# Dilated attention: transposing q and k whole and splitting them out of PSUM, with the second stack of q written by DMA

## The chip, the core and the metric

The kernel runs on one core of a Trainium2 chip. The metric is the device time of one launch in microseconds. A core has five engines with instruction queues of their own: TensorE (PE; PEld is its weight load), VectorE (DVE), ScalarE (ACT), GpSimd (POOL) and SyncE (SP), which here only issues DMAs. Each engine works through its queue in order and waits there for what an instruction needs.

## The reference

Two layers of an encoder over 1024 rows of 1024 numbers in fp32: latent attention with an MLP, then dilated attention with an MLP. The change lies in the dilated attention:

```python
proj = (h @ w_in).reshape(B, S, N_DIL_GROUPS, 3, DIL_HEADS, DIL_HEAD_DIM)   # 3 groups, 16 heads of 64
for gi, (window, dilation) in enumerate(DIL_GROUPS):      # (128, 1), (512, 4), (2048, 16)
    q = rms_norm(proj[:, :, gi, 0], g_q[gi])              # norm over the 64 numbers of a head
    k = rms_norm(proj[:, :, gi, 1], g_k[gi])
    v = proj[:, :, gi, 2]
    o, lse = dilated_group(q, k, v, pos, table, window, dilation)
...
wts = jax.nn.softmax(jnp.stack(lses, axis=0), axis=0)
o = jnp.einsum('gbsh,gbshd->bshd', wts.astype(o_all.dtype), o_all)
```

Within a group a row attends to 64 rows at each side of it (at the distance of the dilation), with a bias per head and distance. The results of the three groups are merged with the denominators of their softmaxes.

## The kernel before, in words

**The stage.** The dilated stage is the method `dil`. It goes through the three groups, in each through eight pairs of heads (a pair is a unit), and in each unit through four steps `tp`; a step makes q and k of two tiles of 128 rows for the pair. That makes 96 steps. Between two groups one empty step permutes the activations for the next dilation (`permute`, copies on ScalarE, VectorE and GpSimd).

**Precision.** A product in nearly full fp32 is made from halves: x is written as hi + lo, both in the type fp32r, hi being x rounded to it and lo the rest. A projection takes three matmuls per block (hi hi, hi lo, lo hi; lines 414 to 416). The scores use stacks instead: for one head the 128 partitions of a tile hold 64 rows of hi and 64 rows of lo. Matmul 0 multiplies the stack of k (hi over lo) with a stack of q that has hi over lo, matmul 1 with one that has lo over hi. Their sum in PSUM has all four products.

**One step, before.** `project` makes the two tiles of q and k of the pair (psproj; 48 matmuls for a tile). `qkstep` forms the norm: squares on ScalarE (dsq, L1825), the sum on VectorE, then qn = psproj times the reciprocal root. On qn, 128x512 (tile, then q of head 0 and 1, then k of head 0 and 1), VectorE multiplies the q half by the product of the two norm weights (gain, L1832). ScalarE copies hi into the first third of `st` (L1834), VectorE writes lo into the second (L1835), and GpSimd copies the q part of hi into the last (L1838), so that hi, lo, hi lie side by side. One step later `stacks` takes windows of 128 columns from it: hi|lo is one stack, lo|hi the other. TensorE transposes them, eight of q (psq, L1847) and four of k (psk, L1855), and ScalarE copies the results to SBUF: two tiles `q` (L1850) and a stretch of `kT` (L1856), which holds the key stacks of the unit.

**After the stacks.** `scores` (L1878) multiplies the q stacks of a tile with 256 key columns around it, four matmuls a tile, into pss; SP loads the tile's bias for it (`bt`, three buffers, L1871). A tile can be scored once the keys behind it are there, so in a unit the two tiles 2 tp - 1 and 2 tp come ready with step tp. VectorE adds the bias and takes the maximum, ScalarE takes the exponential (pd, L1889), `ptrans` transposes the probabilities (pspt, L1904) into pT hi (ScalarE, L1906) and lo (VectorE, L1907), and `av` multiplies with V (psav, L1919 and 1920) and adds up into U on VectorE (L1921, a TENSOR_REDUCE).

**What goes beside.** SP loads weights of two units ahead (wqkr, four loads of 256 KB a unit, L1547) which ScalarE and VectorE split into wqkh (L121) and wqkl (L122) in front of each unit; V is loaded and split per two units. In the third group, when a unit ends, SP brings the U of the first two groups back (`um`, L2024, eight DMAs) and VectorE merges (`merge`, L1989 and 1991, ten instructions); `emit` transposes the merged U (psot, L2008) one step later and stores it to oTd. Where the stage ends, oT is loaded again from oTd for the output projection.

**What orders it.** The Python loop above the step writes out, in this order: V of the step before (`av`), the split of the coming weights, the projection of the first tile, `ptrans`, the um loads, `scores`, `stacks` of two steps back, `emit`, the projection of the second tile, `qkstep`. A list scheduler of the framework then fixes the order on each engine's queue from the dependences; at run time an engine doesn't leave that order. Tiles in PSUM come from one pool of eight banks (psD).

Of the kernel before, what the change touches and what calls it, by code (L numbers as in the profile page):

```python
# [9 lines left out]
F32 = mybir.dt.float32  # L10
F32R = mybir.dt.float32r
# [3 lines left out]
AF = mybir.ActivationFunctionType  # L15
ALU = mybir.AluOpType
# [4 lines left out]
P = 128  # L21
D = 1024
S = 1024
# [18 lines left out]
class K:  # L42
# [1702 lines left out]
    def dil(self, at0, at1, tail, wqk, vd):  # L1745


        nc, a, tc = self.nc, self.a, self.tc
        ctx = ExitStack()
        mkp = lambda name, bufs: ctx.enter_context(tc.tile_pool(name=name, bufs=bufs, reuse_waits="tile"))  # L1750
        dpool = mkp("dil", 2)
        psp = ctx.enter_context(tc.tile_pool(name="psD", bufs=8, space=PSUM, reuse_waits="tile"))
        D_ = lambda name, shape, dt, bufs: dpool.tile(list(shape), dt, tag=name, bufs=bufs, name=self.nm(name))
        PS = lambda name, dt=F32: psp.tile([P, 512], dt, tag="b", name=self.nm(name))
        identr = dpool.tile([P, P], F32R, name="identr", bufs=1)
        nc.vector.tensor_copy(identr, self.ident)
# [62 lines left out]
        def qkstep(u, tp, ps):  # L1819

            g = u["g"]
            p8 = ps.rearrange("p (n e) -> p n e", e=64)
            sq = self.T("dsq")
            ms = self.sm("dms", 8)
            nc.scalar.activation(sq, ps, AF.Square, scale=0.125)  # L1825
            nc.vector.tensor_reduce(ms, sq.rearrange("p (n e) -> p n e", e=64), op=ALU.add, axis=AX.X)
            r = self.rstd(ms, 8, "dr")
            qn = self.T("qn")
            q8 = qn.rearrange("p (n e) -> p n e", e=64)
            nc.vector.tensor_tensor(q8, p8, r.unsqueeze(2).broadcast_to([P, 8, 64]), op=ALU.mult)  # L1830
            qq = qn.rearrange("p (i n e) -> p i n e", i=2, e=64)[:, :, 0:2, :]
            nc.vector.tensor_tensor(qq, qq, gain[:, g : g + 1, :].unsqueeze(1).broadcast_to([P, 2, 2, 64]), op=ALU.mult)  # L1832
            st = D_("st", (P, 8, 192), F32R, 1)
            nc.scalar.activation(st[:, :, 0:64], q8, AF.Copy)  # L1834
            nc.vector.tensor_tensor(st[:, :, 64:128], q8, st[:, :, 0:64].bitcast(F32), op=ALU.subtract)  # L1835
            s4 = st.rearrange("p (i n) e -> p i n e", i=2)
            for i in range(2):
                nc.gpsimd.tensor_scalar(s4[:, i, 0:2, 128:192], s4[:, i, 0:2, 0:64].bitcast(F32), 1.0, 1.0,  # L1838
                                        op0=ALU.mult, op1=ALU.mult)
            return s4  # L1840

        def stacks(u, tp, s4):
            for i in range(2):
                ps = PS("psq", F32R)
                for e in range(2):
                    for k in range(2):
                        nc.tensor.transpose(ps[:, (2 * e + k) * P : (2 * e + k + 1) * P],  # L1847
                                            s4[:, i, e, 64 * k : 64 * k + 128], identr)
                q = D_("q", (P, 2, 2, P), F32R, 4)
                nc.scalar.activation(q.rearrange("p e k t -> p (e k t)"), ps.bitcast(F32), AF.Copy)  # L1850
                u["q"][2 * tp + i] = q
            ps = PS("psk", F32R)
            for e in range(2):
                for i in range(2):
                    nc.tensor.transpose(ps[:, (2 * e + i) * P : (2 * e + i + 1) * P], s4[:, i, 2 + e, 0:128], identr)  # L1855
            nc.scalar.activation(u["k"][:, :, 2 * tp * P : (2 * tp + 2) * P],  # L1856
                                 ps.rearrange("p (e t) -> p e t", e=2).bitcast(F32), AF.Copy)

        def span(g, t):
            if g == 2:  # L1860
                return 64, 192
            n = 8 if g == 0 else 2
            return 64 if t % n == 0 else 0, 192 if t % n == n - 1 else 256

        def scores(u, t):
            g, pr = u["g"], u["pr"]
            bt = D_("bt", (P, 2, 256), F32, 3)
            idx = self.even * (8 - t) + t
            src = self.bias[g][bass.ds(idx, 1), 2 * pr : 2 * pr + 2, 0 : P * 256]
            b0, b1 = (64, 192) if g == 2 else (0, 256)  # L1870
            nc.sync.dma_start(out=bt[:, :, b0:b1], in_=src.rearrange("o h (q c) -> q (o h) c", c=256)[:, :, b0:b1])  # L1871
            ps = PS("pss")
            w0 = min(max(P * t - 64, 0), S - 256)
            off = w0 - (P * t - 64)
            q = u["q"].pop(t)
            for e in range(2):
                for k in range(2):
                    nc.tensor.matmul(ps[:, e * 256 : (e + 1) * 256], q[:, e, k, :], u["k"][:, e, w0 : w0 + 256],  # L1878
                                     start=k == 0, stop=k == 1)
# [7 lines left out]
            nc.scalar.activation(nb, stat[:, g, t, 0, 2 * pr : 2 * pr + 2], AF.Identity, scale=-1.0, bias=ln14)  # L1887
            for e in range(2):
                nc.scalar.activation(p[:, e, lo:hi], p[:, e, lo:hi], AF.Exp, bias=nb[:, e : e + 1],  # L1889
                                     accum_out=stat[:, g, t, 1, 2 * pr + e : 2 * pr + e + 1])  # L1890
# [201 lines left out]
        for n, step in enumerate(steps):  # L2092
# [14 lines left out]
            if step is not None:  # L2107
                kind, g, pr, tp = step
                w = wts[(kind, g, pr)]
                if tp == 0:  # L2110
                    units[(g, pr)] = {"g": g, "pr": pr, "q": {}, "V": VSs[(g, pr // 2)],
                                      "k": D_("kT", (P, 2, S), F32R, 2), "U": self.G("U", (P, 8, P), F32)}
                u = units[(g, pr)]
            for x in transposed:
                x[0]["at"] = n
# [2 lines left out]
            if step is not None:  # L2118
                ps = PS("psproj")
# [197 lines left out]
```

## Time and profile before

| | |
|---|---|
| time, median of 3 runs | 3377.55 us (3376.37 to 3378.83) |
| profiled execution, as a run | 3372.89 us |
| its span, first to last instruction | 3371.0 us |
| its mean granted TensorE clock | 0.985 |
| VectorE, ScalarE, GpSimd busy in the span | 74%, 56%, 23% |
| transposes of `st` (first to last) | 1686.7 to 2626.4 us |

A profile shows one execution. The busy lines of the page give, for each engine, busy time, its share of the span and the number of instructions. A row of a group says: line, engine, operation, tile written <- tiles read, shape and type, count | busy time, mean ns of one | idle time of the engine just ahead of them and what ended most of it; rows of the view by tile say min/median/max ns, first and last start, form. A row of the timeline gives start, length, engine, line, operation, count and, in brackets, the wait ahead of it. A row of a chain of waits gives start, length, engine, tile and line: the chain that ended last, followed back from the end. A row by windows gives a stretch, its length, the busy time of PE, PEld, VectorE, ScalarE and GpSimd, then the granted clock, the share of the 16 DMA engines and GB/s.

### The profile page before, as it was taken

The numbers are of one execution on the slowest core, as the hardware profiler recorded it, in microseconds if no ns is written. First come the engines' busy times: TensorE is split into PE (matmuls) and PEld (weight loads), VectorE is DVE, ScalarE is ACT, GpSimd is POOL, SyncE is SP. The second block draws the span as 40 slices with busy tenths as digits, with TensorE's granted clock in tenths as the row PEclk, the third lists the DMA queues.
The fourth block names the chain that finished last, engine by engine and source line by source line (L and its number), as shares of the span: only waits on it lengthen the run. The fifth ranks groups of instructions, "written<-read, shape, count | busy, mean of one in ns | idle before, by whom it ended". The sixth has DMA issues, their size and how long they took to land.

```text
span 3371.0 us, 53254 instructions
## 1 busy us (share of the span) xinstructions
PE 3250.1 (96%) x19046; PEld 2794.4 (83%) x19046; DVE 2480.3 (74%) x4492; ACT 1877.2 (56%) x3798; POOL 767.5 (23%) x1173
## 2 busy tenths in 40 slices
PE   6989999999999999899999999999999799999999
PEld 6877677688887888778899989998999688887887
DVE  6677777648877866787677787777888578778666
ACT  5547777835544434532267787777667355444342
POOL 6455565520111000011222232222211001110000
PEclk9999999999999999999999999999999899999999
DMA  5453232253655796456433333343334735438564
GB/s 184 129 169 95 92 105 81 84 157 111 224 180 209 244 302 205 162 175 206 143 92 108 101 104 105 113 114 92 104 117 127 208 107 194 153 129 315 198 202 129
DMA packets 385305, 511.31 MB, mean 152 GB/s; under 512 B 37605, under 2 KB 267410, under 8 KB 385034
## 3 DMA queue, kind: packets, MB, share of 16 engines
q1 hardware_dynamic: 357674, 416.53, 40.1%
q0 software_dynamic: 27360, 91.31, 7.3%
q8 instruction: 152, 2.49, 0.3%
q14 instruction: 119, 0.97, 0.1%
HBM read 376.17 MB, written 132.62 MB: 151 GB/s over the span
## 4 chain that ended last, share of the span: by engine, by line
PE 52%; DVE 3%; DMA 1%; ACT 1%; issue 1%; SPq 0%; DVEq 0%; POOL 0%; ACTq 0%; POOLq 0%
PE psm L415 6%; PE psm L416 6%; PE psm L414 6%; PE psproj L414 5%; PE psproj L415 5%; PE psproj L416 5%; PE pss L1878 2%; PE pspt L1904 2%; PE psv L415 2%; PE psv L416 2%; PE psv L414 2%; PE psq L1847 2%; PE psav L1919 2%; PE psav L1920 1%; PE psy L414 1%
## 5 line engine op out<-in xcount | busy, mean ns | idle before, releaser
L415 PE MATMUL psm<-dl,dh 128*128 128x512 f32 x896 | 351.7, 393 | 8.8 <-DVE dl L122 8.7
L414 PE MATMUL psm<-hf,wf 128*128 128x512 f32 x896 | 349.5, 390 | 2.6 <-ACT wf L121 2.6
L416 PE MATMUL psm<-dh,dl 128*128 128x512 f32 x896 | 351.1, 392 | 0.0
L415 PE MATMUL psm<-hf,wf 128*128 128x512 f32 x896 | 348.6, 389 | 0.0
L416 PE MATMUL psm<-hf,wf 128*128 128x512 f32 x896 | 346.6, 389 | 0.4 <-DVE wf L122 0.4
L414 PE MATMUL psm<-dh,dh 128*128 128x512 f32 x896 | 335.0, 391 | 4.5 <-ACT dh L121 4.5
L414 PE MATMUL psproj<-wqkh,hTp 128*128 128x256 f32 x1024 | 301.0, 294 | 0.0
L416 PE MATMUL psproj<-wqkh,hTp 128*128 128x256 f32 x1024 | 292.2, 285 | 0.0
L415 PE MATMUL psproj<-wqkl,hTp 128*128 128x256 f32 x1024 | 292.0, 285 | 0.0
L121 ACT ACTIVATE dh<-ufr 128x1024 fp32r<-128x1024 f32 x112 | 118.4, 1057 | 176.3 <-PE psm L416 50.1
L415 PEld LDWEIGHTS psm<-dl,dh 128*128 128x128 f32 x896 | 169.4, 189 | 46.7 <-DVE dl L122 11.5
L414 PEld LDWEIGHTS psm<-dh,dh 128*128 128x128 f32 x896 | 168.7, 189 | 41.6 <-ACT dh L121 6.6
L414 PEld LDWEIGHTS psm<-hf,wf 128*128 128x128 f32 x896 | 168.2, 188 | 39.9 <-ACT wf L121 5.5
L416 PEld LDWEIGHTS psm<-dh,dl 128*128 128x128 f32 x896 | 169.5, 189 | 35.2
L416 PEld LDWEIGHTS psm<-hf,wf 128*128 128x128 f32 x896 | 168.2, 188 | 35.9 <-DVE wf L122 1.1
L415 PEld LDWEIGHTS psm<-hf,wf 128*128 128x128 f32 x896 | 168.2, 188 | 34.6
L415 PEld LDWEIGHTS psproj<-wqkl,hTp 128*128 128x128 f32 x1024 | 196.3, 192 | 0.0
L414 PEld LDWEIGHTS psproj<-wqkh,hTp 128*128 128x128 f32 x1024 | 195.7, 191 | 0.0
L416 PEld LDWEIGHTS psproj<-wqkh,hTp 128*128 128x128 f32 x1024 | 195.6, 191 | 0.0
L122 DVE TENSOR_TENSOR dl<-ufr,dh 128x1024 fp32r<-128x1024 f32 x112 | 136.6, 1220 | 76.8 <-ACT dh L121 58.1
L745 DVE TENSOR_REDUCE mx<-pmx 128x1 f32<-128x512 f32 x256 | 165.0, 682 | 27.5 <-PE pmx L743 27.3
L1838 POOL TENSOR_SCALAR st<-st 128x128 fp32r<-128x128 f32 x192 | 96.3, 518 | 369.4 <-ACT st L1834 319.2
(401 smaller groups left out, 9458.6 us busy)
## 6 DMA issues: line engine op xcount, KB each, us to landing
ufr<-uf SPq DMA_DIRECT2D x112, 512.0 KB
adaw<-in_ada_w SPq DMA_DIRECT2D x96, 512.0 KB
w2r<-in_mlp_w SPq DMA_DIRECT2D x96, 512.0 KB
w1r<-in_mlp_w SPq DMA_DIRECT2D x64, 512.0 KB
bt<-bias SPq DMA_DIRECT2D x128, 256.0 KB
wqkr<-in_dil_w_in SPq DMA_DIRECT2D x96, 256.0 KB
qkv<-st SPq DMA_DIRECT2D x32, 512.0 KB
hraw<-qkv SPq DMA_DIRECT2D x32, 512.0 KB
```

The costliest lines, as they stand in the source:

```text
L121: nc.scalar.activation(hi, src, AF.Copy)
L122: (lo_eng or nc.vector).tensor_tensor(lo, src, hi.bitcast(F32), op=ALU.subtract)
L414: mm(out, lh, rh, start=first, stop=False)
L415: mm(out, lh, rl, start=False, stop=False)
L416: mm(out, ll, rh, start=False, stop=last)
L745: nc.vector.tensor_reduce(maxes[h][:, 2 * j + b : 2 * j + b + 1], ps, op=ALU.max, axis=AX.X)
L1838: nc.gpsimd.tensor_scalar(s4[:, i, 0:2, 128:192], s4[:, i, 0:2, 0:64].bitcast(F32), 1.0, 1.0, op0=ALU.mult, op1=ALU.mult)
L1847: nc.tensor.transpose(ps[:, (2 * e + k) * P : (2 * e + k + 1) * P], s4[:, i, e, 64 * k : 64 * k + 128], identr)
L1878: nc.tensor.matmul(ps[:, e * 256 : (e + 1) * 256], q[:, e, k, :], u["k"][:, e, w0 : w0 + 256], start=k == 0, stop=k == 1)
L1904: nc.tensor.transpose(ps[:, (n * e + b) * P : (n * e + b + 1) * P], p[:, e, c : c + P], self.ident)
L1919: nc.tensor.matmul(o, pT[:, 0, c], v, start=b == 0, stop=False)
L1920: nc.tensor.matmul(o[:, 0:128], pT[:, 1, c], v[:, 0:128], start=False, stop=b == n - 1)
```

## The change

q and k are no longer split before the transposition, but behind it.

- `qkstep`: the multiplication by the norm weights moves to GpSimd (it stays 128x256); the copy to hi (L1834), lo (L1835) and the two GpSimd copies (L1838) go, with the tile `st`.
- `stacks`: four transposes of qn itself, 128x128, plain fp32, with the identity `ident`, go into one bank psq: first k of both tiles, then q of both. Head e is in partitions 64 e to 64 e + 63. For each head ScalarE writes hi (64x2x256: the keys' columns and the q columns, L1846 of the kernel after) into `kT`, which has 512 columns more for q, and VectorE writes lo into the other 64 partitions (L1847, one input in PSUM). For head 0 that gives hi over lo, for head 1 lo over hi, for k and q alike: q's first stack.
- q's second stack, with the halves swapped, is the tile `qs` (three buffers): two DMAs of 64x2x256 fp32 (128 KB each) from `kT`, issued by SP (L1850), one for each half.
- `scores` takes the weights of matmul 0 from `kT` and those of matmul 1 from `qs`. The fp32r identity `identr` goes.

```diff
+            nc.gpsimd.tensor_tensor(qq, qq, gain[...], op=ALU.mult)          # was nc.vector
+            return qn
-            st = D_("st", (P, 8, 192), F32R, 1)
-            nc.scalar.activation(st[:, :, 0:64], q8, AF.Copy)
-            nc.vector.tensor_tensor(st[:, :, 64:128], q8, st[:, :, 0:64].bitcast(F32), op=ALU.subtract)
-            for i in range(2):
-                nc.gpsimd.tensor_scalar(s4[:, i, 0:2, 128:192], s4[:, i, 0:2, 0:64].bitcast(F32), 1.0, 1.0, ...)
...
-            for i in range(2):
-                ps = PS("psq", F32R)                       # 4 transposes of st each, then:
-                nc.scalar.activation(q.rearrange("p e k t -> p (e k t)"), ps.bitcast(F32), AF.Copy)
-            ps = PS("psk", F32R)                           # 4 transposes of st, then:
-            nc.scalar.activation(u["k"][:, :, 2 * tp * P : (2 * tp + 2) * P], ...)
+            ps = PS("psq")
+            for k in range(2):
+                for i in range(2):
+                    c = i * 256 + (1 - k) * P
+                    nc.tensor.transpose(ps[:, (2 * k + i) * P : (2 * k + i + 1) * P], qn[:, c : c + P], self.ident)
+            q0 = S + tp % 2 * 256
+            qs = D_("qs", (P, 2, 256), F32R, 3)
+            for e in range(2):
+                n, m = (slice(64 * x, 64 * x + 64) for x in (e, 1 - e))
+                s1 = 4 + tp % 2
+                pair = lambda r: u["k"][r, e, :].rearrange("p (s x) -> p s x", x=256)[:, tp : s1 + 1 : s1 - tp, :]
+                x = ps[n, :].rearrange("p (k x) -> p k x", k=2)
+                nc.scalar.activation(pair(n), x, AF.Copy)
+                nc.vector.tensor_tensor(pair(m), x, pair(n).bitcast(F32), op=ALU.subtract)
+            for r in range(2):
+                n, m = (slice(64 * x, 64 * x + 64) for x in (r, 1 - r))
+                nc.sync.dma_start(out=qs[n].bitcast(F32), in_=u["k"][m, :, q0 : q0 + 256].bitcast(F32))
...
-                    nc.tensor.matmul(..., q[:, e, k, :], u["k"][:, e, w0 : w0 + 256], ...)
+                    nc.tensor.matmul(..., q[k][:, e, :], u["k"][:, e, w0 : w0 + 256], ...)
...
-                                      "k": D_("kT", (P, 2, S), F32R, 2), ...
+                                      "k": D_("kT", (P, 2, S + 512), F32R, 2), ...
```

**Order on TensorE.** A late step of the first group, at the scores and the transposes; pspt are the probabilities' transposes, pss the scores, psq and psk the transposes of q and k, psproj the projection of the second tile. Before:

```order
L1904 MATMUL pspt_25390<-ident,pd_25248 128x128 x4
L1878 MATMUL pss_25400<-kT_24521,q_25112 128x256 x4
L1878 MATMUL pss_25414<-kT_24521,q_25260 128x256 x4
L1847 MATMUL psq_25426<-identr,st_25159 128x128 x4
L1847 MATMUL psq_25433<-identr,st_25159 128x128 x4
L414 MATMUL psproj_25357<-wqkh_25021,hT_3811_18667 128x256
...
L414 MATMUL psproj_25357<-wqkh_25025,hT_3860_18891 128x256
L1855 MATMUL psk_25440<-identr,st_25159 128x128 x4
```

and after:

```order
L1899 MATMUL pspt_25027<-ident,pd_24898 128x128 x4
L1873 MATMUL pss_25037<-kT_24223 128x256
L1873 MATMUL pss_25037<-kT_24223,qs_24768 128x256
...
L1873 MATMUL pss_25051<-kT_24223 128x256
L1838 MATMUL psq_25063<-ident,qn_24811 128x128 x4
L414 MATMUL psproj_24994<-wqkh_24684,hT_3811_18667 128x256
...
L415 MATMUL psproj_24994<-wqkl_24685,hT_3836_18782 128x256
L1873 MATMUL pss_25051<-kT_24223,qs_24910 128x256
L1873 MATMUL pss_25051<-kT_24223 128x256
```

The twelve transposes have become four, and the second tile's scores (pss_25051) are pulled apart: their first matmul stands ahead of the next step's transposes, the first one that reads the stack qs_24910 stands behind them and behind eleven projection matmuls.

**Order on ScalarE.** The step ahead of it; pT are the probabilities' hi, dnb and pd the maxima and exponentials of two tiles, dsq the squares of the next step. Before:

```order
L1906 ACTIVATE pT_25224<-pspt_25219 128x512
L1850 ACTIVATE q_25260<-psq_25255 128x512
L1850 ACTIVATE q_25267<-psq_25262 128x512
L1834 ACTIVATE st_25159<-qn_25156 128x8x64
L1856 ACTIVATE kT_24521<-psk_25269 128x2x256
L1887 ACTIVATE dnb_25237<-stat,ln_20892 128x2
L1887 ACTIVATE dnb_25251<-stat,ln_20892 128x2
L1889 ACTIVATE pd_25234,stat<-pd_25234,dnb_25237 128x256 x2
L1889 ACTIVATE pd_25248,stat<-pd_25248,dnb_25251 128x256 x2
L1825 ACTIVATE dsq_25299<-psproj_25186 128x512
```

and after:

```order
L1901 ACTIVATE pT_24874<-pspt_24869 128x512
L1846 ACTIVATE kT_24223<-psq_24905 64x2x256
L1882 ACTIVATE dnb_24887<-stat,ln_20890 128x2
L1884 ACTIVATE pd_24884,stat<-pd_24884,dnb_24887 128x256 x2
L1882 ACTIVATE dnb_24901<-stat,ln_20890 128x2
L1884 ACTIVATE pd_24898,stat<-pd_24898,dnb_24901 128x256 x2
L1846 ACTIVATE kT_24223<-psq_24905 64x2x256
L1822 ACTIVATE dsq_24941<-psproj_24836 128x512
```

Four copies have become two half as high, and the second of them (head 1) stands behind the exponentials of both tiles. By the framework's dependences it also waits for VectorE's subtraction of head 0. On VectorE the subtraction of head 1 stands behind a reduction into U:

```order
L1878 ISA pd_24898,stat<-pss_24893,bt_24891 128x256
L1878 ISA stat 128x1
L1847 TENSOR_TENSOR kT_24223<-psq_24905,kT_24223 64x2x256
L1916 TENSOR_REDUCE U_23627<-psav_24973 128x128
L1847 TENSOR_TENSOR kT_24223<-psq_24905,kT_24223 64x2x256
```

The chain of a step's stacks is now hi of head 0, lo of head 0, hi of head 1, lo of head 1, and then the DMAs that swap the halves.

**Order on SyncE.** The same place of the first group: bt are bias loads, U a store, wqkr weight loads. Before:

```order
L1871 DMA bt_25412<-bias_135 128x2x256
L1871 ISA
L1871 DMA bt_25551<-bias_135 128x2x256
L1547 DMA wqkr_25643<-in_dil_w_in 128x4x128
L1937 DMA U<-U_23873 128x8x128
```

and after:

```order
L1866 DMA bt_25035<-bias_135 128x2x256
L1850 DMA qs_24768<-kT_24223 64x2x256 x2
L1866 ISA
L1866 DMA bt_25049<-bias_135 128x2x256
L1866 ISA
L1866 DMA bt_25175<-bias_135 128x2x256
L1850 DMA qs_24910<-kT_24223 64x2x256
L1932 DMA U<-U_23627 128x8x128
L1850 DMA qs_24910<-kT_24223 64x2x256
L1547 DMA wqkr_25254<-in_dil_w_in 128x4x128 x2
```

Both DMAs of a step's second stack stand in the same queue as the loads, the second one here behind the store of U. At a unit's end in the third group they stand among the loads of um:

```order
L1866 DMA bt_31514<-bias_137 128x2x128
L2019 DMA um_31650<-U 64x4x128
L1850 DMA qs_31265<-kT_30504 64x2x256
L2019 DMA um_31650<-U 64x4x128
L1850 DMA qs_31265<-kT_30504 64x2x256
L2019 DMA um_31650<-U 64x4x128
L2019 DMA um_31655<-U 64x4x128 x4
```

More of the change, by code (lines that the diff above doesn't have):

```diff
@@ L1840, in qkstep @@
-            return s4
-        def stacks(u, tp, s4):
-            for i in range(2):
-                ps = PS("psq", F32R)
[L1845 to L1851, printed above, removed]
-            ps = PS("psk", F32R)
-            for e in range(2):
-                for i in range(2):
-                    nc.tensor.transpose(ps[:, (2 * e + i) * P : (2 * e + i + 1) * P], s4[:, i, 2 + e, 0:128], identr)
-            nc.scalar.activation(u["k"][:, :, 2 * tp * P : (2 * tp + 2) * P],
-                                 ps.rearrange("p (e t) -> p e t", e=2).bitcast(F32), AF.Copy)
+            nc.gpsimd.tensor_tensor(qq, qq, gain[:, g : g + 1, :].unsqueeze(1).broadcast_to([P, 2, 2, 64]), op=ALU.mult)
@@ new lines, in qkstep, with stacks @@
+            return qn
+        def stacks(u, tp, qn):
+            ps = PS("psq")
[15 more added lines that the diff above has]
+                nc.sync.dma_start(out=qs[n].bitcast(F32), in_=u["k"][m, :, q0 : q0 + 256].bitcast(F32))
+            for i in range(2):
+                u["q"][2 * tp + i] = (u["k"][:, :, q0 + i * P : q0 + (i + 1) * P], qs[:, :, i * P : (i + 1) * P])
@@ L2111, in dil @@
                     units[(g, pr)] = {"g": g, "pr": pr, "q": {}, "V": VSs[(g, pr // 2)],
[L2112 removed]
+                                      "k": D_("kT", (P, 2, S + 512), F32R, 2), "U": self.G("U", (P, 8, P), F32)}
                 u = units[(g, pr)]
```

8 lines of the change are left out of this document (1 added, 7 removed).

## The prediction

> **What bounds the kernel now.** I read the page first, then stretches of the dilated stage, then the chain of work that ended last. The first two lines are the page's; the rows below them are stretches of the stage: start and end, length, then busy time of each engine, the granted TensorE clock, the DMA share and GB/s.
>
> ```profile
> span 3371.0 us, 53254 instructions
> PE 3250.1 (96%) x19046; PEld 2794.4 (83%) x19046; DVE 2480.3 (74%) x4492; ACT 1877.2 (56%) x3798; POOL 767.5 (23%) x1173
> ```
>
> ```profile
> 2040.00:2090.00 50.00, 50.00 (x475) 49.66 (x474) 36.27 (x102) 34.86 (x104) 14.14 (x29) 1.00 0.37 109
> 2480.00:2520.00 40.00, 35.29 (x310) 34.58 (x309) 33.57 (x104) 28.62 (x88) 5.64 (x12) 0.94 0.46 132
> 1968.00:1990.00 22.00, 13.81 (x110) 12.78 (x108) 19.67 (x35) 19.93 (x42) 9.13 (x9) 0.77 0.31 84
> 2625.00:2650.00 25.00, 13.24 (x79) 10.94 (x79) 21.79 (x57) 9.88 (x28) 0.00 (x1) 0.64 1.04 320
> ```
>
> In the first two groups of heads (2040 to 2090 stands for them) TensorE is never idle, while VectorE and ScalarE are busy 73% and 70%: there, time taken off TensorE is time taken off the kernel. In the third group (2480 to 2520) VectorE is busy 84% and TensorE already loses 4.7 us of 40. Between two groups (1968 to 1990) the permuting copies fill ScalarE and VectorE, and at the end (2625 to 2650) the DMA engines are full.
>
> The chain of work, in order of time, gives the length of a step: from the scores of one to the scores of the next.
>
> ```profile
> 2045.13 0.95 PE pss L1878 x8
> 2054.99 0.95 PE pss L1878 x8
> ...
> 2570.45 0.95 PE pss L1878 x8
> 2579.31 0.95 PE pss L1878 x8
> ```
>
> A step is 9.8 us in the first groups and 8.9 in the third. There are 96 steps, 32 in each group, four to a unit (a pair of heads).
>
> **TensorE, the gain.** In the same chain, a place where nothing waits:
>
> ```profile
> 2599.82 0.12 PE psproj L416
> 2599.94 0.64 PE psq L1847 x8
> 2600.58 0.34 PE psk L1855 x4
> 2600.93 0.89 PE psot L2008 x8
> ```
>
> The twelve fp32r transposes of a step take 0.64 + 0.34 = 0.98 us of TensorE's time. They go. Four transposes of plain F32 data come instead; the eight of psot are of that kind and take 0.89, so four take 0.44. A step saves 0.54 us and 96 steps save 52 us, if nothing comes late. The score matmuls stay eight of 256 columns; only where their weights lie changes.
>
> **The other engines.** Groups of the stage by line and shape: count, then busy time, mean ns of one, idle time before.
>
> ```profile
> L1850 ACT ACTIVATE q<-psq 128x512 fp32r<-128x512 f32 x190 | 104.7, 594 | 31.8 <-PE psq L1847 31.5
> ...
> L1838 POOL TENSOR_SCALAR st<-st 128x128 fp32r<-128x128 f32 x190 | 95.3, 518 | 369.4 <-ACT st L1834 319.2 <-PE psav L1920 35.8 <-DVE wqkl L122 11.4
> L1907 DVE TENSOR_TENSOR pT<-pspt,pT 128x512 f16<-128x512 f32 x128 | 87.9, 687 | 24.9 <-ACT pT L1906 24.4
> ...
> L1835 DVE TENSOR_TENSOR st<-qn,st 128x512 fp32r<-128x512 f32 x95 | 68.7, 723 | 31.7 <-ACT st L1834 31.3
> ...
> L1834 ACT ACTIVATE st<-qn 128x512 fp32r<-128x512 f32 x95 | 59.9, 630 | 16.4 <-DVE qn L1832 11.2 <-PE psk L1855 2.7 <-POOL vs L1815 1.6
> L1856 ACT ACTIVATE kT<-psk 128x512 fp32r<-128x512 f32 x95 | 56.3, 592 | 3.0 <-PE psk L1855 2.7
> ...
> L122 DVE TENSOR_TENSOR wqkl<-wqkr,wqkh 128x1024 fp32r<-128x1024 f32 x44 | 53.9, 1225 | 7.8 <-ACT wqkh L121 7.6
> ...
> L1832 DVE TENSOR_TENSOR qn<-qn,dgain 128x256 f32<-128x256 f32 x94 | 48.0, 510 | 1.2
> ...
> L121 ACT ACTIVATE wqkh<-wqkr 128x1024 fp32r<-128x1024 f32 x44 | 46.8, 1064 | 11.3 <-DMA wqkr<-in_dil_w_in 11.2
> ```
>
> ScalarE loses 630 + 2 x 594 + 592 = 2410 ns a step and gets two copies of 64x512, which I price by the 594 of 128x512: it gains 1.22 us a step. That hides behind TensorE, so it is worth nothing but a shorter queue. VectorE loses 510 + 723 and gets two subtractions with one input in PSUM, 687 each by L1907: 0.14 us more a step, also hidden in the first groups. GpSimd loses two copies (518 each) and gets the multiplication by the norm weights. Half as wide as q and k, it is nearest to this row of GpSimd:
>
> ```profile
> 2092.61 0.67 POOL L1815 TENSOR_TENSOR vs<-vr,vs 128x256 bf16<-128x256 f32 x1
> ```
>
> So 0.67, bounded by 0 and by 1.04 (the two copies that go); a whole step lies between it and its reader, and I take nothing. The dropped identr copy is one instruction, nothing too.
>
> The Trainium skill's page "SBUF — State Buffer", section "Who interferes with whom", says that a VectorE instruction with two SBUF inputs and a GpSimd instruction that reads SBUF block each other. No row here separates that cost; by the page the multiplication, now on GpSimd, could hold up VectorE in the third group, which is the third rival below.
>
> **The new wait.** The second stack of q now exists only after a chain: copy of one head's hi, its lo, the other head's hi, its lo, then two DMAs. The order shows that the second copy stands on ScalarE behind the exponentials of both tiles, and the second subtraction on VectorE behind a U reduction. Durations, from one step of before (timeline rows: start, us, engine):
>
> ```profile
> 2095.03 0.79 PE L1847 MATMUL psq<-identr,st 128*128 128x128 f32 x8
> ```
>
> ```profile
> 2095.52 1.09 ACT L1850 ACTIVATE q<-psq 128x512 fp32r<-128x512 f32 x2 [0.60 <-PE psq L1847]
> 2096.49 0.29 ACT L1887 ACTIVATE dnb<-stat,ln 128x2 f32<-128x2 f32 x1
> 2096.82 0.46 ACT L1889 ACTIVATE pd<-pd,dnb 128x192 f32<-128x192 f32 x1
> ...
> 2097.62 0.19 ACT L1889 ACTIVATION_READ_ACCUMULATOR pd<-pd,dnb 128x1 f32 x1
> ```
>
> ```profile
> 2099.73 0.56 DVE L1921 TENSOR_REDUCE U<-psav 128x128 f32<-128x384 f32 x1 [0.20 <-PE psav L1920]
> ```
>
> Counted from the start of the transposes: the first hi begins at 2095.52 - 2095.03 = 0.49 and ends at 1.08. One tile's exponentials take 2096.49 to 2097.81, 1.32, two take 2.64: 3.72. The second hi ends at 4.31. The U reduction began at 4.70 in before, 0.54 earlier now: 4.16 to 4.72. The last lo ends at 5.4. Then the DMA, SBUF to SBUF, 128 KB, of which before has no example. The nearest rows are a store that SP waits for (last figure: longest, 2.2 us), and the landing of the last of eight 128 KB loads of um in the chain:
>
> ```profile
> SPq L1956 <- DMA S<-stat: 3.8, 2, 2.2
> ```
>
> ```profile
> 2428.94 3.16 DMA um<-U
> ```
>
> I take 2.7, in the middle of 2.2 and 3.2: both are about its size, one alone and one in a queue. The chain ends at 8.1 (7.6 to 8.6). Its first reader on TensorE stands behind the next transposes: 9.8 - 0.54 + 0.44 = 9.7. So the ordinary step of the first groups has 1.6 us to spare and keeps the 0.54.
>
> The Trainium skill's page "DMA: Bandwidth & Descriptors", section "Anatomy of one DMA", gives about 2.0 us fixed plus the bytes at 436 GB/s, for another issuing path. By it this DMA would take 2.3 us, an estimate, inside the rows' bounds; the 24 late steps counted next would each be 0.4 us less late, and the sum 37 us instead of 27.
>
> What runs over: (a) once a unit the weights are split, 2 x 1.06 us on ScalarE and 2 x 1.23 on VectorE. That puts the chain at 9.8 by ScalarE alone and at 12.3 with VectorE's share too, while the order has up to 11 projection matmuls of 0.12 (1.3 us) in front of the reader there (the rows of TensorE shown with the change). Short by 0 to 1.3; I take 0.4, nearer to the case of one engine, for 16 units: 6 us. (b) In the third group, VectorE's merge and SP's loads of um come once a unit.
>
> ```profile
> L2024 SPq DMA_DIRECT2D um<-U x64: 573/614/1232, 2361.6 to 2634.3; - x64
> L1989 DVE TENSOR_TENSOR um<-um,mgf x32: 677/685/771, 2385.4 to 2646.3; 128x512 f32<-128x512 f32 x32
> ```
>
> Five merge instructions of 0.685 ahead of a subtraction add 3.4; eight loads issued over 8 x 0.61 = 4.9 us ahead of the stack's DMA add about 3. The chain is then 14.5, against 8.9 - 0.54 + 0.44 = 8.8, and up to 13 projection matmuls in between (1.6): short by 4.1 at worst, 0 at best. I take 1.8, because both queues are seldom long in one step: 8 units, 14 us. (c) Where a group ends there are no projections behind which to wait: two subtractions and a DMA, 4.1 us, come on top of what ScalarE did, against about 2.4 us that it has less to do in two steps. I take 2 us at each of two ends. At the end of the stage the last stacks' DMA is queued among these reloads:
>
> ```profile
> 2623.57 10.07 DMA oT<-oTd
> ```
>
> TensorE waits for the same reloads already, so the bounds are 0 and 10; I take 1, near the end where it is hidden. Together 5.
>
> SP gets 192 more DMAs; those that wait hold up the bias loads behind them, which have a third buffer and about a step of lead, so I take nothing; if that cover goes, it is the second rival.
>
> **Sum**: -52 + 6 + 14 + 5 = -27 us. The profiled execution took 3372.89 as a run (its span is 3371.0), so 3345.9; the median of the runs is 3377.55, 4.7 above it, and I forecast **3350.5** on that scale.
>
> **Rivals.** *All of it hidden*: as the forecast, but merges and loads fall where they hurt nobody: -52, 3325.5. For it: TensorE's 100% in 2040 to 2090. Against: the third group's 84% VectorE. Chance 0.2. *The stack is late in every step* (slower): queued with bias, weights and V loads its DMA takes 3 us more, 5.7. The chain is 11.1, the ordinary step is short by 1.4, and with TensorE's idle time the clock falls too: 1968 to 1990 has 0.77. Two chains overlap, since the next transposes stand ahead of the wait, so at least half is paid each step, 0.7; with the clock I take 0.8: 96 x 0.8 = 77, less 52: +25, 3402.5. It decides from 0.54 us a step on. For it: the loads in a queue (3.16 and 10.07). Against: DMA share 0.37 in the first groups. Chance 0.2. *GpSimd blocks VectorE*: in the third group each of 32 multiplications holds a merge up by 0.67: 21 us, so -6, 3371.5. For it: L1838 takes 518 in the mean, far over its shortest of 290 (row below), so something does hold GpSimd up. Against: the two VectorE instructions that go had two SBUF inputs as well. Chance 0.1. The forecast has 0.5, from 3336 to 3370.
>
> ```profile
> L1838 POOL TENSOR_SCALAR st<-st x192: 290/299/1292, 1686.1 to 2624.3; 128x128 fp32r<-128x128 f32 x192
> ```
>
> **Range and chances.** A measurement of this kernel can tell about 0.2%, 6.8 us, from no change: 3370.8 to 3384.3. Faster 0.7 (forecast and all hidden), same 0.1, slower 0.2. The range reaches from 3322, just below the case in which all is hidden, to 3398, just below that of a late stack in every step: it leaves out the upper half of the slow case, about 0.1, and little else.
>
> **What would show it.** Right: in 2040 to 2090 TensorE still at 100%, steps of about 9.3 us, psq groups of four in 0.44 us; waits of TensorE for a DMA on qs, small in sum and mostly after 2300, about 14 us; ScalarE 1.2 us less busy a step. Wrong: waits of pss for qs in most steps, steps over 9.8; subtractions from psq far from 0.69, or transposes of qn far from 0.11; the multiplication on GpSimd over 1.04.

## The result

The kernel after the change takes **3350.28 us** (median of 4 runs, 3349.55 to 3353.20), the kernel before beside it 3377.65 us (3376.37 to 3378.83). The ratio is 0.9921, with a 95% interval of 0.9903 to 0.9938: 27 us faster. The profiled execution took 3350.56 us, its span is 3348.8 us, its mean clock 0.981.

The busy lines of the page of the kernel after:

```profile
span 3348.8 us, 52027 instructions
PE 3201.8 (96%) x18278; PEld 2737.9 (82%) x18278; DVE 2521.1 (75%) x4491; ACT 1810.8 (54%) x3606; POOL 749.9 (22%) x1077
```

TensorE has 48 us less to do, ScalarE 66 us less, and VectorE 41 us more. Stretches of the same times as before (columns as before: start and end, length, busy PE, PEld, VectorE, ScalarE, GpSimd, clock, DMA share, GB/s); the kernel after is some 15 and 30 us further on in its work at these times:

```profile
2040.00:2090.00 50.00, 49.58 (x451) 49.16 (x450) 40.93 (x113) 34.42 (x98) 13.70 (x28) 1.00 0.52 140
2480.00:2520.00 40.00, 32.31 (x267) 31.55 (x265) 34.70 (x98) 21.55 (x68) 6.84 (x7) 0.91 0.58 165
```

In the first groups TensorE is still nearly full (49.58 of 50), and VectorE has gone from 36 to 41 us of 50. Over the longer stretch from 1990 to 2280 the DMA share has gone from 0.39 to 0.50; without the new transfers (an experiment below) it is 0.38 there. In the third group, where TensorE had lost 4.7 us of 40, it now loses 7.7. The new operations, groups of the stage (count, then busy time, mean ns, idle time ahead):

```profile
L1847 DVE TENSOR_TENSOR kT<-psq,kT 64x512 fp32r<-64x512 f32 x192 | 132.2, 688 | 23.8 <-ACT kT L1846 18.3
...
L1846 ACT ACTIVATE kT<-psq 64x512 fp32r<-64x512 f32 x191 | 112.6, 590 | 46.1 <-PE psq L1838 29.2 <-DVE kT L1847 11.0 <-issue 2.5
...
L1873 PE MATMUL pss<-kT,qs 128*128 128x256 f32 x384 | 108.7, 301 | 15.6 <-DMA qs<-kT 15.2
...
L1829 POOL TENSOR_TENSOR qn<-qn,dgain 128x256 f32<-128x256 f32 x94 | 81.5, 867 | 593.6 <-DVE qn L1827 491.8 <-ACT pT L1901 34.4 <-ACT pd L1884 17.1
```

The subtraction takes 0.688 us, the copy to hi 0.590, the multiplication on GpSimd 0.867, and the wait of the scores for the second stack comes to 15 us in the whole stage.

To see where the time went, TensorE's records between the squares (dsq) of the first and of the last step are summed by tile, each matmul counted from its start to the start of the next; where that is over 0.45 us, all but 0.12 us of it is counted as a pause. The last two columns are two of the experiments below.

| us | before | after | without the second stack | second stack by GpSimd |
|---|---|---|---|---|
| first to last squares | 934.5 | 903.7 | 879.4 | 887.9 |
| transposes of q and k | 91.0 | 35.4 | 35.8 | 35.2 |
| score matmuls | 99.6 | 104.6 | 100.7 | 102.8 |
| pauses | 28.0 | 51.4 | 34.5 | 39.3 |
| all else | 715.9 | 712.3 | 708.4 | 710.6 |

The transposes give 55.6 us. The pauses take back 23.4, and the score matmuls, which now are pulled apart and wait a little, 5.0.

### The profile page after: what moved, and what is told of

Its sections match the earlier page's. It is cut to its first block, busy times and chain, and to the rows that moved or that the text cites. A ratio compares the mean times of both kernels' runs of the same rounds, so it can differ in the third digit from the quotient of the medians.

```text
span 3348.8 us, 52027 instructions
## 1 busy us (share of the span) xinstructions
PE 3201.8 (96%) x18278; PEld 2737.9 (82%) x18278; DVE 2521.1 (75%) x4491; ACT 1810.8 (54%) x3606; POOL 749.9 (22%) x1077
## 5 line engine op out<-in xcount | busy, mean ns | idle before, releaser
L1829 POOL TENSOR_TENSOR qn<-qn,dgain 128x256 f32<-128x256 f32 x96 | 83.5, 870 | 596.0 <-DVE qn L1827 494.2
```

Of the source, the lines that this page charges most:

```text
L1829: nc.gpsimd.tensor_tensor(qq, qq, gain[:, g : g + 1, :].unsqueeze(1).broadcast_to([P, 2, 2, 64]), op=ALU.mult)
```

## The experiments

After the result there were these theories. **A**: what the transposes gave was partly given back because of the second stack of q; **A1** by its landing, which TensorE waits for, **A2** by its place in SP's queue, which holds up other loads. **B**: VectorE, with wider work and the merges, has become the bound of the third group. **C**: GpSimd blocks VectorE. Each kernel was compared with runs of the kernel before on the same chip (medians 3374.3 to 3375.5). Beside the kernel after, the kernel before had 3377.65, so a difference of medians from the kernel after can be off by some 3 us; the ratios to the kernel before allow for that.

The scheduler orders each kernel anew, so an edit also moves instructions that it doesn't name. How much one trace says is seen from the first two groups of the kernel after and of the two variants that are edited only in the third: 615.5, 612.6 and 612.2 us.

| from the first squares of the stage, us | first two groups | third group up to the output projection | of it to the last projection matmul | the end |
|---|---|---|---|---|
| before | 644.4 | 328.5 | 290.0 | 38.5 |
| before, without additions | 644.4 | 331.2 | 288.9 | 42.3 |
| after | 615.5 | 333.7 | 286.5 | 47.2 |
| without the second stack | 605.3 | 320.4 | 273.4 | 46.9 |
| DMAs issued, not read | 607.6 | 328.7 | 279.2 | 49.5 |
| second stack by GpSimd | 606.6 | 325.6 | 279.2 | 46.4 |
| after, multiplication on VectorE | 616.3 | 340.4 | 290.9 | 49.5 |
| after, without additions | 612.2 | 326.2 | 278.9 | 47.2 |
| after, additions on GpSimd | 612.6 | 343.7 | 293.9 | 49.9 |

**Without the second stack.** The two DMAs and the tile qs go:

```diff
-            for r in range(2):
-                nc.sync.dma_start(out=qs[n].bitcast(F32), in_=u["k"][m, :, q0 : q0 + 256].bitcast(F32))
-                u["q"][2 * tp + i] = (u["k"][:, :, ...], qs[:, :, i * P : (i + 1) * P])
+                u["q"][2 * tp + i] = (u["k"][:, :, ...],) * 2
```

> The changed kernel without the second stack of q: no tile qs, no DMA for it, both score matmuls read kT (this leaves out the cross products hi lo and lo hi of the scores). Theory A: what the change gave back after its 55.6 us on the transposes was given back because of the second stack (its DMA's landing, its share of SP's queue): TensorE's waits in the first two groups (about 8 us), the 7 us at the end of the stage and some 5 of the third group return, 3330. Rival B: in the third group VectorE, with its merges and the wider subtractions, is the bound and the second stack only lies beside it: not more than 8 us return, 3342 or above.

Measured: 3328.27 us (3325.40 to 3329.96), ratio 0.9865 (0.9850 to 0.9880): 22 us below the kernel after (19 by the ratios), as theory A had it. The windows of this kernel:

```profile
2040.00:2090.00 50.00, 50.00 (x457) 49.74 (x456) 41.27 (x114) 35.66 (x96) 11.68 (x26) 1.00 0.48 135
2480.00:2520.00 40.00, 39.43 (x349) 39.11 (x347) 38.88 (x104) 26.52 (x82) 9.46 (x10) 1.00 0.38 117
```

TensorE is full again in the first groups. In the second window (which holds another part of the third group) VectorE has 38.88 of 40 us to do: it is the engine next to the bound. The table of stretches puts 10 us of the second stack's cost in the first two groups and 13 in the third, all of them ahead of its last projection matmul, where 5 were expected. Another expectation fell: the **end of the stage** did not get shorter. From the last projection matmul to the output projection it takes 38.5 us before, 47.2 after and 46.9 here. TensorE's waits there (us in sum, times, longest), first after, then without the second stack:

```profile
PE pss L1873 <- DMA qs<-kT: 7.8, 4, 4.2
PE psot L2003 <- DVE U L1986: 5.1, 2, 4.1
PE pspt L1899 <- ACT pd L1884: 4.3, 2, 2.5
```

```profile
PE psot L1999 <- DVE U L1982: 10.0, 3, 3.6
PE pspt L1895 <- ACT pd L1880: 7.9, 5, 3.4
```

The waits for qs are there to be seen (7.8 us), and with their cause taken away, waits for VectorE's merges and for the exponentials stand in their place.

**The DMAs issued but not read.** Only the last line of that edit: qs is written, the scores read kT twice.

> The changed kernel with the two DMAs per step issued as they are, but qs not read: both score matmuls read kT (this leaves out the cross products of the scores). It splits the cost of the second stack, 19 to 25 us by the run without it. Theory A1, the landing counts: TensorE waits for qs, and without a reader the time is that of the run without the DMAs, 3329. Theory A2, SP's queue counts: the DMAs wait there for the subtractions and hold up bias, um and weight loads behind them: then most of it stays, 3343 to 3350. From the waits of TensorE for qs, 15 us in the trace, of which not all is on the way to the end: I expect 3335.

Measured: 3339.61 us (3338.49 to 3341.05), ratio 0.9894 (0.9879 to 0.9910), in the middle between the kernel after and the one without DMAs. So A1, the landing that TensorE waits for, is worth about 10 us, and about 10 us stay without a reader; the intervals of neighbours just touch, so the halves are rough. In the first two groups nearly all goes with the reader (607.6 of 615.5 to 605.3), in the third, up to the last projection matmul, 7.3 of the 13.1. That the rest is SP's queue (A2) is not shown: the kernel with GpSimd copies, which clears that queue of these DMAs, takes the same 279.2 us there, and between 2315 and 2570 VectorE waits for um 1.8 us here and 0.2 us in the kernel after. The DMAs' traffic beside the other loads, and the new order of the queues, are rivals that no run separates.

**The second stack by ScalarE, by GpSimd, and by both.** The DMA is replaced by a copy:

```diff
-                nc.sync.dma_start(out=qs[n].bitcast(F32), in_=u["k"][m, :, q0 : q0 + 256].bitcast(F32))
+                nc.scalar.activation(qs[n], u["k"][m, :, q0 : q0 + 256].bitcast(F32), AF.Copy)      # ScalarE
+                nc.gpsimd.tensor_scalar(qs[n], u["k"][m, ...].bitcast(F32), 1.0, 1.0, ...)          # or GpSimd
```

> The changed kernel with the second stack of q written by two ScalarE copies of 64x512 per step, from kT to qs, instead of two DMAs. Theory A: ScalarE has the room (54% busy), two copies are 1.2 us in place of a DMA of 2.5 us and more, and SP's queue is shorter: 3336. Rival B: the copies stand on ScalarE behind the exponentials and hold up the copies and exponentials behind them, above all in the third group: 3350 or slower.

> The second stack by two GpSimd copies of 64x512 per step in place of the DMAs. GpSimd is 22% busy; the copies wait for the last subtraction and stand in front of the next multiplication by the norm weights. If they take 0.3 to 0.9 us each and block nobody, the time is that of the two ScalarE copies or less, 3333 to 3340. Rival C, GpSimd with SBUF operands blocks VectorE: 64 x 2 copies in the third group and its end, 3345 or slower.

> One half of the second stack by a ScalarE copy, the other by a GpSimd copy, side by side. If what is left with two ScalarE copies (12 us above the run without a second stack) is the time of the copies in ScalarE's queue, half of it goes: 3334. If it is VectorE that bounds the third group, nothing changes: 3340.

Measured: ScalarE 3340.15 us (3337.40 to 3341.95), ratio 0.9897 (0.9882 to 0.9912); **GpSimd 3333.45 us** (3328.27 to 3333.92), ratio 0.9870 (0.9855 to 0.9886); one half each 3335.53 us (3333.33 to 3339.24), ratio 0.9884 (0.9868 to 0.9899). All three medians are below the change as made (the interval of the ScalarE copies still overlaps that of the change, and the order among the three is not clear of noise), and the copies on GpSimd beat both kernels: 42 us below before and 17 below after. A group of that kernel:

```profile
L1850 POOL TENSOR_SCALAR qs<-kT 64x512 fp32r<-64x512 f32 x192 | 125.5, 654 | 325.2 <-ACT kT L1846 242.5 <-DVE kT L1847 52.1 <-issue 23.2
```

A copy takes 0.654 us in the mean, where the DMA took 2.47 in the median from issue to the last of its 16 completions (2.32 to 7.82; 39 of 192 over 3.0), and SP's queue is free of it. The engine had the room: GpSimd was 22% busy.

**The same DMAs from ScalarE's queue.**

```diff
-                nc.sync.dma_start(out=qs[n].bitcast(F32), ...)
+                nc.scalar.dma_start(out=qs[n].bitcast(F32), ...)
```

> The changed kernel with the same two DMAs issued from ScalarE's queue in place of SP's. Theory A2 (SP's queue): SP is free of them, so the loads behind come in time, and it gets faster, 3340. But ScalarE then waits in its queue for VectorE's last subtraction and issues for some 0.1 to 0.6 us each: if that costs more than the SP queue did, 3355 or slower. I expect 3350, no difference from the changed kernel.

Measured: 3364.48 us (3362.14 to 3365.97), ratio 0.9967 (0.9955 to 0.9979): 14 us slower than from SP. My expectation of no difference was wrong. TensorE's wait for the stack in the first two groups (1690 to 2290), first after, then here:

```profile
PE pss L1873 <- DMA qs<-kT: 6.8, 11, 1.0
```

```profile
PE pss L1873 <- DMA qs<-kT: 12.6, 11, 2.1
```

The wait has nearly doubled, and the landing has grown to 3.05 us in the median. In ScalarE's queue each issue takes about 0.6 us, and by the order of the queue what stands behind it can start only after the subtraction that the DMA waits for. How the 14 us divide between this and the later landing was not taken apart.

**The multiplication by the norm weights.** Back on VectorE in the kernel after, and alone on GpSimd in the kernel before:

```diff
-            nc.gpsimd.tensor_tensor(qq, qq, gain[...], op=ALU.mult)
+            nc.vector.tensor_tensor(qq, qq, gain[...], op=ALU.mult)
```

> The changed kernel with the multiplication by the norm weights back on VectorE. Theory A: VectorE is a bound only in the third group: 32 multiplications of 0.51, of which a third to a half shows: +5 to +8, about 3357; nothing in the first two groups. Rival C: GpSimd, multiplying in SBUF, blocks VectorE: then it gets faster, 3345 or below.

> The kernel before with only the multiplication by the norm weights moved to GpSimd, one part of the change alone. Theory A: worth nothing in the first two groups, up to 4 us in the third, where VectorE is 84% busy, less what the longer way to hi (0.87 on GpSimd in place of 0.51) costs: 3372 to 3378, about no change. Rival C: GpSimd blocks VectorE and is itself late, since it has the two copies of hi still to do: 3385 or slower.

Measured: 3357.02 us (3353.51 to 3358.18) for the first, ratio 0.9947 (0.9933 to 0.9960), 7 us slower than the change; 3377.35 us (3373.11 to 3383.71) for the second, ratio 1.0007 (0.9998 to 1.0016), no change. So the move to GpSimd is worth nothing by itself, and in the kernel after some 7 us (9 by the ratios, whose intervals overlap a little: the direction is clearer than the size). By the table 4.4 of them lie in the third group up to the last projection matmul; that VectorE is tight there is the likely reason, not a tested one.

**VectorE in the third group.** First the additions of the merges on GpSimd, in all units but the last, in the kernel after and in the one with GpSimd copies:

```diff
-                    nc.vector.tensor_tensor(U, U, y, op=ALU.add)
+                    (nc.gpsimd if u["pr"] < 7 else nc.vector).tensor_tensor(U, U, y, op=ALU.add)
```

> The changed kernel, and in the third group the 28 additions of the merges (U = U + um, all units but the last) on GpSimd in place of VectorE, 28 x 0.69 = 19 us less for VectorE there. Theory A+B: some 10 us of the third group are lost because VectorE is full at the merges, so about 8 come back: 3342. Rival A alone, only the second stack counts: no change, 3350. Rival C, GpSimd blocks VectorE with two SBUF operands: slower, 3356.

> Second stack by GpSimd copies (3333 before) and these 28 additions on GpSimd too. Theory A+B: what is left in the third group is VectorE's: 3325. Rival C: GpSimd, now with copies, multiplications and additions, is late with the second stack at the merges or blocks VectorE: 3333 or slower.

Measured: 3358.87 us (3354.87 to 3360.51), ratio 0.9950 (0.9936 to 0.9963), and 3341.75 us (3340.57 to 3343.96), ratio 0.9899 (0.9884 to 0.9914): both some 8 us slower than without the edit. I had expected 8 us faster; slower is what rival C said. VectorE's merge multiplications in the third group, after and with the additions on GpSimd, and these additions themselves (min/median/max):

```profile
L1984 DVE TENSOR_TENSOR um<-um,mgf 128x512 f32<-128x512 f32 x32 | 23.5, 758 | 1.1 <-DMA um<-U 1.0
```

```profile
L1984 DVE TENSOR_TENSOR um<-um,mgf 128x512 f32<-128x512 f32 x32 | 32.5, 1042 | 1.5 <-DMA um<-U 1.4
```

```profile
L1986 POOL TENSOR_TENSOR U<-U,um x28: 1262/1286/1697, 2350.7 to 2607.0; 128x512 f32<-128x512 f32 x28
```

Not only do 28 additions take 1.29 us each on GpSimd in place of 0.69; the 32 multiplications on VectorE take 1.04 in the mean in place of 0.76, and each of the 15 that took over 0.8 ran beside an instruction of GpSimd. 19 us of work were taken off VectorE, and the sum of its instructions in the third group and its end didn't fall (334 us after, 335 here). The edit therefore couldn't decide on B. The additions were then left out:

```diff
-                if k < 2:
+                if k < 2 and u["pr"] == 7:
                     nc.vector.tensor_tensor(U, U, y, op=ALU.add)
```

> The changed kernel with the additions of the merges left out in all units of the third group but the last (28 instructions of VectorE, 19 us; the groups are then not summed for these heads): VectorE is relieved without GpSimd's help. Theory B, VectorE's merges bound the third group of the changed kernel: some 10 us come back, 3340. Rival A, only the second stack counts: within 3 us of 3350.

> The same additions left out of the kernel before, as the control: TensorE lost 10 us in gaps in its third group. Theory B: the bound of VectorE is new with the change, so less comes back here than there: 3 to 6 us, 3370. If as much or more comes back here, the merges were a bound already and the change has not made them one.

Measured: 3340.00 us (3338.11 to 3346.87), ratio 0.9907 (0.9892 to 0.9922), for the kernel after; 3378.41 us (3374.51 to 3381.38), ratio 1.0009 (1.0000 to 1.0018), for the kernel before. Relief of VectorE gives 7.6 us in the third group of the kernel after by the traces (286.5 to 278.9), 10 us between the medians and 5 by the ratios, whose intervals overlap; before, it gives 1.1 us in the trace and nothing in the time. So the traces speak for theory B, VectorE as a bound of the third group that is new with the change, but the size, some 5 to 10 us, is not clear of noise. It may also overlap with what the second stack costs there: with fewer additions ahead of the subtractions the chain that writes that stack is shorter too. How it looks: VectorE of the kernel after at the end of a unit, 2402 to 2409.

```profile
2402.75 0.69 DVE L1984 TENSOR_TENSOR um<-um,mgf 128x512 f32<-128x512 f32 x1
2403.35 0.42 DVE L1902 TENSOR_TENSOR pT<-pspt,pT 128x256 f16<-128x256 f32 x1
2403.68 0.68 DVE L1827 TENSOR_TENSOR qn<-psproj,dry 128x512 f32<-128x512 f32 x1
2404.28 0.69 DVE L1986 TENSOR_TENSOR U<-U,um 128x512 f32<-128x512 f32 x1
2404.88 1.22 DVE L1984 TENSOR_TENSOR um<-um,mgf 128x512 f32<-128x512 f32 x1
2406.02 0.68 DVE L1986 TENSOR_TENSOR U<-U,um 128x512 f32<-128x512 f32 x1
2406.62 0.68 DVE L1984 TENSOR_TENSOR um<-um,mgf 128x512 f32<-128x512 f32 x1
2407.22 0.68 DVE L1823 TENSOR_REDUCE dms<-dsq 128x8 f32<-128x512 f32 x1
2407.82 0.28 DVE L1878 CUSTOM_DVE_ANT_0 pd<-pss,bt 128x128 f32<-128x128 f32 x1
```

and what GpSimd and TensorE do beside it:

```profile
2404.51 1.03 POOL L1829 TENSOR_TENSOR qn<-qn,dgain 128x256 f32<-128x256 f32 x1 [8.70 <-DVE qn L1827]
```

```profile
2409.24 0.47 PE L1899 MATMUL pspt<-ident,pd 128*128 128x128 f32 x1 [5.08 <-ACT pd L1884]
```

TensorE stands still for 5.08 us. The wait is put down to ScalarE's exponentials, but those wait for the bias addition on VectorE (L1878 at 2407.82), and that stands behind five merge instructions and three others without a gap. One of them took 1.22 in place of 0.69, while the multiplication by the norm weights ran on GpSimd.

## Why the prediction came out right, step by step

**The transposes (52 us): right.** They gave 55.6 us, 0.58 a step: twelve took 91.0 / 96 = 0.95 and four take 0.37 in place of 0.44.

**The new operations: right but for one.** 0.688 for the subtraction (0.687 forecast), 0.590 for the copy (0.594). The multiplication on GpSimd takes 0.867 in the mean, not 0.67, but inside the bounds (0.739 in the median; single ones took up to 1.27), and it lies beside other work as said: putting it back costs some 7 us. *Failed in size* is VectorE's load: "0.14 us more a step" is what the exchange gives in durations (132.2 in, 48.8 + 70.3 out: 13 us), but the page has 41 us more of busy time. 16 of them are lost overlap: successive VectorE instructions lay over each other by 118 us in sum before and by 102 after (1680 to 2620). The other 11 are VectorE instructions that the change doesn't name and that took longer, most of all the merges' multiplications of um (2.3). ScalarE falls short the other way: 1.22 us a step would be 117 us less, and the page has 66, because its instructions lay over each other by 238 us in sum before and by 180 after (whole run).

**The landing: right.** 2.47 us in the median where I took 2.7 between 2.2 and 3.2; in the longest case 7.82, which my bounds of 2.2 and 3.2 did not hold (39 of 192 took over 3.0). The term of the chain was the time from the last subtraction until both halves have landed; in the first two groups it is 2.98 in the median.

**The first two groups (6 us lost): right.** By step 64 x 0.58 = 37.1 us should have come and 28.9 came (644.4 to 615.5). So 8 were lost, where the sum had 6 here and 4 at the two group ends. TensorE pauses for the stack in 11 of the 64 steps, for about 1 us or less, 6.8 us in sum. Counted by the step whose stack it waits for, five pauses (2.6 us) belong to the last step of a unit, four (2.4 us) to the first step and two to a third step. The split of the weights is what sets the last step apart: in 12 of the 16 units it puts 3 to 4.6 us of ScalarE's and VectorE's time into that step's chain. There the chain ends 10.9 us behind the start of the transposes in the median and its reader stands at 11.4; in the other steps the chain ends at 8.6 to 8.8 (forecast 8.1) and the reader stands at 9.6 to 9.7 (forecast 9.7). This is the forecast's mechanism, and its place for five of the eleven. No run moved the split.

**The third group (14 us lost): right in size, but not by the path that was forecast.** Up to the last projection matmul 32 x 0.58 = 18.6 us should have come and 3.5 came (290.0 to 286.5), so 15 were lost, and 13.1 of these come back without the second stack. But they were to be lost in TensorE's waits for a late stack, once in each of 8 units. TensorE's waits from 2315 to 2600, first the two largest before, then all after:

```profile
PE pspt L1904 <- ACT pd L1889: 4.4, 2, 2.4
PE psav L1919 <- ACT pT L1906: 2.5, 2, 2.3
```

```profile
PE pspt L1899 <- ACT pd L1884: 13.4, 3, 5.9
PE psav L1914 <- ACT pT L1901: 6.0, 5, 1.7
PE psav L1915 <- DVE pT L1902: 4.0, 6, 1.5
PE pss L1873 <- DMA qs<-kT: 1.9, 3, 1.0
PE psproj L414 <- DVE stat L1878: 1.6, 2, 0.8
```

The waits for qs are small. Those for the exponentials (pd) and for the probabilities (pT) have grown, and the exponentials wait for the bias addition on VectorE. The sum had VectorE's merges only as something that makes the stack late; as work that holds up the exponentials, as in the stretch from 2402 to 2409 above, it had no term for them. The additions (7.6) and the second stack (13.1) together are more than the 15 us lost, so they are not two separate costs. Of the second stack's part 7.3 us go when nothing reads it; by which waits the second stack costs the rest is open.

**Where groups end, and the end of the stage (5 us): wrong in its parts.** At the two group ends nothing was lost: the four steps around each took 53.6 and 52.0 us before and take 51.6 and 49.8 now, about 4 x 0.58 = 2.3 less, and TensorE's long pause there stays at 8 to 9 us. At the end of the stage 8.7 us were lost where I took 1, and not by the last stacks' DMA, which was my reason: without it the end is as long. In the traces of two variants of the kernel before (the multiplication alone moved, and the additions left out in all units but the last) this end took 42.6 and 42.3 us, so 4 of the 8.7 may be chance in the one trace of before. What holds the rest is open.

**The rivals.** All hidden (-52 us) is nearly what the kernel without the second stack comes to: 46.6 us below the kernel before on its chip. A late stack in every step (3402.5) didn't come, because the chain has spare time in most steps, though less than the forecast gave it: 1.0 us in the median of the first two groups in place of 1.6. GpSimd blocking VectorE is there, but small in this change: the merges' multiplications went from 33.0 to 35.3 us in sum. It is larger where GpSimd adds whole tiles (0.76 to 1.04 us in the mean of the 32). The Trainium skill's page "SBUF — State Buffer", section "Who interferes with whom", states that a VectorE instruction with two SBUF inputs contends with a GpSimd instruction that reads SBUF; the trace agrees in direction. The change itself takes VectorE out of this at one place. The subtraction had two SBUF inputs before and has one in PSUM now:

```profile
L1835 DVE TENSOR_TENSOR st<-qn,st x96: 634/693/1562, 1685.1 to 2624.1; 128x512 fp32r<-128x512 f32 x96
```

```profile
L1847 DVE TENSOR_TENSOR kT<-psq,kT x192: 683/690/694, 1689.4 to 2600.6; 64x512 fp32r<-64x512 f32 x192
```

Single ones took up to 1.562 us before (min/median/max in ns); now none takes over 0.694, although 35 of the 192 run beside GpSimd for over 0.3 us.

**The sum.** The forecast of 3350.5 and the 3350.28 measured agree to a fraction of what either is worth. From profiled run to profiled run the change is -22.3 us (3372.89 to 3350.56), not -27; the profiled execution of before lay 4.7 under its median, that of after lies at its own. By stretches of the two traces the first two groups got 28.9 us shorter (the forecast's terms give 24.6), the third up to its last projection matmul 3.5 (3.3), the end 8.7 longer (1), and what lies ahead of the stage 1.5 longer. So the traces fall 4.7 us short of the sum: the end cost 7.7 us more than forecast and the first two groups gave 4.3 more. The offset of 4.7 that was added for the median makes up for that. If the short end of before is chance, as the two variants suggest, both may be the same 4 us. That the two numbers agree to 0.2 us is luck; that they agree within some 5 is not.

## What to carry to other kernels

Time taken off the bounding engine is kept only as far as the engines and queues beside it have spare time at that place: 55.6 us came off TensorE, some 30 went back, 15 of them in the third group, where a second engine was already 84% busy, and up to 9 where the stage ends. For a small rearrangement inside SBUF, compare a DMA's landing (2.47 us, and a share of the issue queue) with a copy on an idle engine (0.654 us): here the copy was worth another 17 us. Before work is moved to an idle engine, look at what it does to its neighbour: additions on GpSimd made VectorE's multiplications over a third longer in the mean, and the kernel 8 us slower.

## What the runs showed of the hardware

A DMA of 128 KB inside SBUF landed in 2.47 us in the median and in up to 7.82 near the end of the stage, among weight, um and oT loads. From ScalarE's queue it landed in 3.05 us in the median, and its issue took 0.6 us there as on SP. A GpSimd copy of 64x512 took 0.654 us in the mean, one on ScalarE 0.63. An addition of two 128x512 tiles took 1.29 us on GpSimd and 0.69 on VectorE. A VectorE subtraction with one input in PSUM took 0.683 to 0.694 us in all 192 cases; with both in SBUF it took 0.634 to 1.562. Successive instructions of VectorE overlap in the trace, by 118 us in sum before and 102 after (1680 to 2620), so busy time moves by another amount than the durations that were exchanged.
